# Two token blocks multiplied before their norm, and the second norm's scalings moved behind the residual sums

## The chip, the cores and the metric

The kernel runs on one core of one Trainium2 chip. The metric is the device time of one execution in microseconds; runs before and after are compared by their medians. Each profile is one execution taken by the hardware profiler. Its engines are TensorE (PE; its weight loads are listed apart as PEld), VectorE (DVE), ScalarE (ACT), GpSimd (POOL) and SyncE (SP), and its times count from the first instruction of the span.

## The reference

One decoder layer over 512 tokens of 1024 channels, in float32. What matters here is its beginning and its middle:

```python
u = _rmsnorm(h, norm1_g[l])
proj = u @ w_in[l]
a_glu, q, k, v, r, g_low, gate_a, gate_b = _split_cols(proj)
...
merged = jax.nn.sigmoid(gate_a) * y_conv + jax.nn.sigmoid(gate_b) * y_gla
h = h + merged @ w_o[l]

u2 = _rmsnorm(h, norm2_g[l])
z = _causal_dwconv(u2 @ w_ffn_up[l], ffn_dw_w[l], ffn_dw_b[l])
h = h + (jax.nn.silu(z[..., :FFN_DIM]) * z[..., FFN_DIM:]) @ w_ffn_down[l]
```

`_rmsnorm` multiplies each token by one over the root of its mean square plus 1e-6, and each channel by a gain. The token's factor is common to all channels, so it can be applied to a product's row as well as to the factor that goes into it; the gain can't.

## The kernel before

Tokens lie in four blocks of 128 (`NT` = 4), channels in eight of 128 (`KT` = 8). Every float32 matrix is split in two, a high part (ScalarE casts it to `F32R`: `uh` of activations, `whi` of weights) and a low part, what is left (VectorE subtracts: `ul`, `wlo`). A product takes three TensorE instructions (`mm3`, L288 to L294): activation low by weight high, high by low, high by high. Sums accumulate in PSUM, five banks of tag `mm` and three of tag `ax`. A weight tile is half a megabyte; `load` (L160) issues its DMA on SyncE's queue into one of four `raw` tiles, and `split_weight` (L220) makes `whi` and `wlo` and issues the next load.

**The start** (L377 to L443) runs under an order written out by hand for TensorE, ScalarE, VectorE and SyncE: on each of them instructions stand in the order of the program, and each waits for those ahead. The gain row of the first norm lands on one partition. TensorE spreads it over all partitions with `ones` (L398), makes three products of the identity (L402), and then waits. `norm1` (L404) takes the mean square of a block of tokens on ScalarE (L407), adds 1e-6 on VectorE (L409), the power -0.5 on GpSimd (L340), and scales the block by root and gain in place (L413). `to_channels` (L363) turns the block: four transposes into one PSUM bank (L369), the cast (L373), the subtraction (L374), twice. Then `row_half` (L306) multiplies block 0 by the first half of the value weight (four weight tiles `w_v`, 24 products of 512 columns), then block 1, 2, 3; in the middle of each block (`MID`) the next one is turned and the one after it normalised. `v_done` (L435) copies the values out. The normalised, turned blocks `u1` serve all other input projections, the first of which (`w_glu`) follows at once, by `col_tile` (L296), over all 512 tokens.

**The middle.** The output projection `w_o` goes through `seven` (L816): seven products of sums in place of eight, in the order of `STEPS` (L44), each for two token blocks `i` = 0, 1. A product group of step and `i` is 12 instructions of 512 columns. After a group VectorE adds its bank to the residual `hres` (L859); several steps accumulate into the same bank, so that a later step's group begins only when VectorE has read what stands there. Where a half of `hres` is final, `complete` is called (`o_complete`, L892): the square sum, then the root, then `norm2` (L883), two VectorE instructions that scale a block into `un` (L887). `o_at` (L901) is called just before the addition of its step: at n3 it scaled blocks 0 and 1, at a22 it turned them. The order of instructions in this part isn't written out by hand; a scheduler draws it up from the program's order. The feed-forward part then multiplies its first four `w_up` tiles for 256 tokens (blocks 0 and 1), turns blocks 2 and 3 after the third and the fourth of them (L1016 to L1020), and goes on with the other 256.

## Time and profile before

| | |
|---|---|
| median of 3 runs | 849.79 us (849.37 to 850.01) |
| profiled execution | 850.15 us, of which the span is 848.4 us |
| granted TensorE clock, mean | 0.998 |
| instructions in the span | 9947 |
| DMA | 97.79 MB, mean 115 GB/s |

The profile gives busy time by engine, groups of instructions by line, and for each idle stretch of an engine the one that ended it (`<-`). In a timeline a row is: start, length, engine, line, operation, out<-in, partitions x columns, count, and in brackets the idle time ahead and what ended it. Consecutive instructions of one kind are merged into one row with their count. A product's length includes a tail in which the next one already runs; the distance from start to start is what it costs. A float32 product that isn't `F32R` takes two instructions.

### The profile page before, as it was taken

Reading aid. Unit: us, or ns where it says so; the run is one execution under the profiler, and the core shown is the slowest. Engines: PE = TensorE matmul, PEld = TensorE weight load, DVE = VectorE, ACT = ScalarE, POOL = GpSimd, SP = SyncE. Lnnn points to the kernel's source line nnn. Section 1 sums busy time; section 2 is a strip of 40 time slices with the busy share of each in tenths; the row PEclk is TensorE's granted clock in tenths of the full one; section 3 lists DMA queues with packets and bytes.
Section 4 is the critical chain, followed back from the end, with each engine's and each line's share of the span. In section 5 each row is a group of like instructions: output and inputs, shape, how many; then the busy total and the mean of one; then the engine's idle time right before and its main releaser. Section 6 shows DMA issues by size and latency. Waiting matters only on the chain.

```text
span 848.4 us, 9947 instructions
## 1 busy us (share of the span) xinstructions
PE 835.3 (98%) x3814; PEld 691.0 (81%) x3814; DVE 646.1 (76%) x913; ACT 383.3 (45%) x531; POOL 42.6 (5%) x60
## 2 busy tenths in 40 slices
PE   8999999999999999999999999999999999999996
PEld 6888888888888888788888788888888888888885
DVE  5479879999998788744688749778767777677795
ACT  5433336535443422449444526444334443444454
POOL 1000000000100100000001100000100010000011
PEclk9999999999999999999999999999999999999999
DMA  8223232222222322222338533225732238222462
GB/s 288 94 100 104 95 107 81 97 96 81 94 75 75 124 100 99 75 99 75 119 82 228 191 124 126 100 81 118 211 126 99 71 89 273 96 94 98 100 124 101
DMA packets 28579, 97.79 MB, mean 115 GB/s; under 512 B 3233, under 2 KB 3361, under 8 KB 28530
## 3 DMA queue, kind: packets, MB, share of 16 engines
q1 hardware_dynamic: 25074, 85.35, 28.8%
q0 software_dynamic: 3456, 11.80, 7.8%
q8 instruction: 30, 0.49, 0.2%
q14 instruction: 19, 0.16, 0.1%
HBM read 95.03 MB, written 2.10 MB: 114 GB/s over the span
## 4 chain that ended last, share of the span: by engine, by line
PE 96%; DVE 1%; DMA 1%; ACT 1%; issue 0%; POOL 0%; SPq 0%; POOLq 0%; ACTq 0%
PE mm L292 30%; PE mm L293 29%; PE mm L294 29%; PE ax L293 1%; PE ax L294 1%; PE ax L292 1%; PE ax L698 1%; DMA raw<-in_w_v_dram 1%; PE ax L680 1%; PE ax L700 1%; DVE hres L859 0%; PE ax L369 0%; PE ax L667 0%; PE ax L715 0%; PE ax L666 0%
## 5 line engine op out<-in xcount | busy, mean ns | idle before, releaser
L292 PE MATMUL mm<-uh,wlo 128*128 128x512 f32 (+1 forms) x768 | 294.4, 384 | 1.2 <-DVE wlo L250 0.6
L293 PE MATMUL mm<-ul,whi 128*128 128x512 f32 (+1 forms) x768 | 292.0, 381 | 0.2 <-DVE ul L374 0.2
L294 PE MATMUL mm<-uh,whi 128*128 128x512 f32 (+1 forms) x768 | 292.2, 381 | 0.0
L247 ACT CAST whi<-raw 128x1024 fp32r<-128x1024 f32 x116 | 120.8, 1045 | 134.6 <-PE mm L294 101.3
L250 DVE TENSOR_TENSOR wlo<-raw,whi 128x1024 fp32r<-128x1024 f32 x116 | 141.0, 1219 | 38.3 <-ACT whi L247 37.8
L292 PEld LDWEIGHTS mm<-uh,wlo 128*128 128x128 f32 x768 | 144.2, 188 | 29.0 <-ACT uh L373 1.0
L293 PEld LDWEIGHTS mm<-ul,whi 128*128 128x128 f32 x768 | 144.5, 188 | 27.8 <-DVE ul L374 0.6
L294 PEld LDWEIGHTS mm<-uh,whi 128*128 128x128 f32 x768 | 144.4, 188 | 27.9
L457 DVE SCALAR_TENSOR_TENSOR c<-h,pp,c 128x511 f32<-128x511 f32 (+14 forms) x240 | 162.3, 728 | 0.7
L925 DVE SCALAR_TENSOR_TENSOR tmp<-mm,pp,tmp 128x511 f32<-128x511 f32 x88 | 65.8, 748 | 66.0 <-ACT tmp L923 64.8
L923 ACT ACTIVATE tmp<-mm,pp 128x512 f32<-128x512 f32 x44 | 34.3, 780 | 62.9 <-PE mm L294 62.9
L231 ACT CAST whi<-kept 128x1024 fp32r<-128x1024 f32 (+1 forms) x32 | 31.6, 992 | 24.4 <-DVE kept L211 12.8
L232 DVE TENSOR_TENSOR wlo<-kept,whi 128x1024 fp32r<-128x1024 f32 (+1 forms) x32 | 36.6, 1152 | 2.8 <-ACT whi L231 2.8
L859 DVE TENSOR_TENSOR hres<-hres,mm 128x512 f32<-128x512 f32 x48 | 32.6, 682 | 5.6 <-PE mm L294 3.8
L231 ACT CAST whi<-raw 128x1024 fp32r<-128x1024 f32 (+1 forms) x24 | 23.6, 992 | 19.8 <-PE mm L294 19.5
L340 POOL TENSOR_TENSOR rstd<-var,mhalf 128x1 f32<-128x1 f32 (+1 forms) x20 | 17.6, 884 | 262.2 <-DVE var L705 195.6
L232 DVE TENSOR_TENSOR wlo<-raw,whi 128x1024 fp32r<-128x1024 f32 (+1 forms) x24 | 27.3, 1152 | 3.5 <-ACT whi L231 3.5
L292 PE MATMUL mm<-whi,ul 128*128 128x512 f32 x64 | 26.3, 411 | 1.3 <-DVE ul L374 1.3
L293 PE MATMUL mm<-wlo,sh 128*128 128x512 f32 x66 | 26.0, 395 | 0.0
L294 PE MATMUL mm<-whi,sh 128*128 128x512 f32 x66 | 26.0, 394 | 0.0
L292 PE MATMUL mm<-whi,sl 128*128 128x512 f32 x66 | 25.9, 394 | 0.0
L292 PE MATMUL mm<-h,wlo 128*128 128x512 f32 x64 | 25.7, 402 | 0.0
(220 smaller groups left out, 1124.4 us busy)
## 6 DMA issues: line engine op xcount, KB each, us to landing
raw<-in_w_up_dram SPq DMA_DIRECT2D x44, 512.0 KB, 3.3
raw<-in_w_glu_dram SPq DMA_DIRECT2D x16, 512.0 KB, 3.6
raw<-in_w_down_dram SPq DMA_DIRECT2D x15, 512.0 KB, 3.2
kept<-in_w_down_dram POOLq DMA_DIRECT2D x10, 512.0 KB, 5.1
raw<-in_w_v_dram SPq DMA_DIRECT2D x8, 512.0 KB, 3.9
raw<-in_w_qk_dram SPq DMA_DIRECT2D x8, 512.0 KB, 3.2
raw<-in_w_r_dram SPq DMA_DIRECT2D x8, 512.0 KB, 3.3
raw<-in_w_gb_dram SPq DMA_DIRECT2D x8, 512.0 KB, 3.3
```

Of the source, the lines that this page charges most:

```text
L231: nc.scalar.copy(hi, raw)
L232: nc.vector.tensor_tensor(lo, raw, hi.bitcast(F32), ALU.subtract)
L247: nc.scalar.copy(hi, raw)
L250: pace[0] = nc.vector.tensor_tensor(lo, raw, hi.bitcast(F32), ALU.subtract)
L292: nc.tensor.matmul(acc, ll, rh, start=first, stop=False, **kw)
L293: nc.tensor.matmul(acc, lh, rl, start=False, stop=False, **kw)
L294: nc.tensor.matmul(acc, lh, rh, start=False, stop=last, **kw)
L340: nc.gpsimd.tensor_tensor(r, v, mhalf[:, :n], ALU.pow)
L457: nc.vector.scalar_tensor_tensor(y[:, s:], c[:, : T - s], w, y[:, s:], ALU.mult, ALU.add)
L859: nc.vector.tensor_tensor(hres[t, n], hres[t, n], bank[of[step]][i], op)
L923: nc.scalar.activation(z, acc, AF.Identity, bias=pp[:, PP_FB + m : PP_FB + m + 1], scale=w[2])
L925: nc.vector.scalar_tensor_tensor(z[:, s:], acc[:, : T - s], w[j], z[:, s:], ALU.mult, ALU.add)
```

## The change

Five parts.

1. *The gain row.* It is no longer spread over the partitions. Eight one-column products with a single `1.0` turn it into a tile `gains` of channels by partition.
2. *Blocks 0 and 1* (`EARLY` = 2) are turned as they land. The gain is applied by VectorE while it copies the turned block out of PSUM, the parts are cast and subtracted into tiles of their own (`eu`), and the value product is made of these. The token's factor is applied when `v_done` copies the values out. For the later projections, `normalize` multiplies the turned copies by the factor, spread over the partitions by TensorE, and splits them again into `u1`.
3. *Blocks 2 and 3* are scaled by their factor on ScalarE, turned, and given the gain on the way out of PSUM.
4. *The order* of the first value products is written out: high by high first, then high by low, then low by high; blocks 0 and 1 side by side through the four weight tiles, then block 2, then 3. The first two weight tiles are split in halves of 512 columns. `WARM` now counts products of `ones` at four places of TensorE's queue. The loads stand in the order row, block 0, weight 0, block 1, weights 1 and 2, block 2, weight 3.
5. *The second norm.* The scaling of blocks 0 and 1 moves from ahead of the residual's addition in step n3 to behind it, one block behind each addition; their transposes move one product group ahead, to n3's second group and a22's first; in the feed-forward part blocks 2 and 3 are turned after the second and third `w_up` tile.

```diff
@@ -35,8 +35,9 @@
 AHEAD = 4
 LOOK = 2
 RATE = 5.0
-WARM = 3
+WARM = (6, 6, 6, 4)
 MID = 4
+EARLY = 2
 ET = mybir.EngineType
 SEVEN = {"w_o": KT // 2, "w_down": FT // 2}
 
@@ -217,7 +218,8 @@
             nxt = block(name, pairs, d, *((0, 1) if step == "a11" else (1, 0)))
             nc.gpsimd.dma_start(kept[pairs, d], nxt, accum_op=ALU.add)
 
-    def split_weight(between=None):
+    def split_weight(halves=False, between=None):
+
         if len(ready) < len(order):
             while len(raws) <= len(ready):
                 load()
@@ -244,9 +246,17 @@
                 load()
                 return
             lo = wp.tile([P, D], F32R, tag="wlo", name=nm("wlo"), bufs=4)
+            if halves:
+                ready.append((hi, lo))
+
+                def low(c):
+                    nc.vector.tensor_tensor(lo[:, c], raw[:, c], hi[:, c].bitcast(F32), ALU.subtract)
+
+                cols = [slice(j * T, (j + 1) * T) for j in range(2)]
+                for c in cols:
+                    nc.scalar.copy(hi[:, c], raw[:, c])
+                return [lambda c=c: low(c) for c in cols]
             nc.scalar.copy(hi, raw)
-            if between:
-                between()
             pace[0] = nc.vector.tensor_tensor(lo, raw, hi.bitcast(F32), ALU.subtract)
             ready.append((hi, lo))
             load()
@@ -374,72 +384,211 @@
             nc.vector.tensor_tensor(ul, tr3, uh.bitcast(F32), ALU.subtract)
 
 
+
+
     u1 = new_acts()
-    row = tp.tile([P, D], F32, tag="gain", name=nm("row"), bufs=1)[0:1, :]
+    acts1 = by_k(u1)
     nc.vector.memset(ones, 1.0)
     nc.gpsimd.memset(mhalf, -0.5)
-    xs = {}
+    xs, rs, xg, eu = {}, {}, {}, {}
 
     def load_x(t):
         xs[t] = tp.tile([P, D], F32, tag="x", name=nm("x"), bufs=3)
         nc.sync.dma_start(xs[t], a["x"][t * P : (t + 1) * P, :])
 
+    def by_four(t):
+        return t.rearrange("p (k t) -> p k t", k=4)
+
     start = tc.manual_schedule(engines=START)
     start.__enter__()
+    row = tp.tile([P, D], F32, tag="gain", name=nm("row"), bufs=1)[0:1, :]
     nc.sync.dma_start(row, a["norm1_g"].unsqueeze(0))
     load_x(0)
     load()
-    load()
     load_x(1)
     load()
-
-    gain1 = [mm_bank(), mm_bank()]
-    for j in range(2):
-        nc.tensor.matmul(gain1[j], ones[0:1, :], row[:, j * T : (j + 1) * T], start=True, stop=True)
-
-    warm = ax_bank()
-    for _ in range(WARM):
-        nc.tensor.matmul(warm[:, :P], ident, ident, start=True, stop=True)
-
-    def norm1(t):
-        xt = xs[t]
+    load()
+    load_x(2)
+    load()
+
+    idle = mm_bank()
+
+    def warm(n):
+        for _ in range(n):
+            nc.tensor.matmul(idle[:, :P], ones, ones, start=True, stop=True)
+
+
+    gains = cp.tile([P, KT], F32, name="gains")
+    warm(WARM[0])
+    for k in range(KT):
+        nc.tensor.matmul(
+            idle[:, P + k : P + k + 1], row[:, k * P : (k + 1) * P], ones[0:1, 0:1], start=True, stop=True
+        )
+    nc.scalar.copy(gains, idle[:, P : P + KT])
+    warm(WARM[1])
+
+    def transposed(x, g):
+        tr = ax_bank()
+        for k in range(4):
+            c = (g * 4 + k) * P
+            nc.tensor.transpose(tr[:, k * P : (k + 1) * P], x[:, c : c + P], ident)
+        return tr
+
+    def with_gain(tr, g):
+        f = heap()
+        by_channel = gains[:, g * 4 : g * 4 + 4].unsqueeze(2).to_broadcast([P, 4, P])
+        nc.vector.tensor_tensor(by_four(f), by_four(tr), by_channel, ALU.mult)
+        return f
+
+    def in_u1(t, g):
+        return [x[:, :, t * P : (t + 1) * P] for x in u1[g]]
+
+    def high(hi, f):
+        nc.scalar.copy(hi, f)
+
+    def low(lo, f, hi):
+        nc.vector.tensor_tensor(lo, f, hi.bitcast(F32), ALU.subtract)
+
+    def squares(t):
         ss = small(1, "ss")
-        nc.scalar.activation(junk(D), xt, AF.Square, scale=1.0 / 32.0, accum_out=ss)
+        nc.scalar.activation(junk(D), xs[t], AF.Square, scale=1.0 / 32.0, accum_out=ss)
+        rs[t] = ss
+
+    def root(t):
         v = small(1, "var")
-        nc.vector.tensor_scalar(v, ss, EPS, None, ALU.add)
-        r = rsqrt(v, 1)
-        for j in range(2):
-            s = slice(j * T, (j + 1) * T)
-            nc.vector.scalar_tensor_tensor(xt[:, s], xt[:, s], r, gain1[j], ALU.mult, ALU.mult)
-
-    norm1(0)
-    split_weight()
-    split_weight(lambda: to_channels(xs[0], u1, 0, (0,)))
-    to_channels(xs[0], u1, 0, (1,))
-    load_x(2)
-    norm1(1)
-    split_weight()
+        nc.vector.tensor_scalar(v, rs[t], EPS, None, ALU.add)
+        rs[t] = tp.tile([P, 1], F32, tag="r1", name=nm("r1"), bufs=NT)
+        nc.gpsimd.tensor_tensor(rs[t], v, mhalf[:, :1], ALU.pow)
+
+    def early_acts(t):
+        for g in range(2):
+            xg[t, g] = transposed(xs[t], g)
+
+    def early_gain(t, g):
+        xg[t, g] = with_gain(xg[t, g], g)
+        eu[t, g] = [by_four(heap(F32R)) for _ in range(2)]
+
+    def early_high(t, g):
+        high(eu[t, g][0], by_four(xg[t, g]))
+
+    def early_low(t, g):
+        low(eu[t, g][1], by_four(xg[t, g]), eu[t, g][0])
+
+    def into_u1(t, fs):
+        for g in range(2):
+            high(in_u1(t, g)[0], fs[g])
+        for g in range(2):
+            hi, lo = in_u1(t, g)
+            low(lo, fs[g], hi)
+
+    def normalize(t, r):
+
+        fs = [by_four(xg[t, g]) for g in range(2)]
+        for f in fs:
+            nc.vector.tensor_tensor(f, f, r[:, t * P : (t + 1) * P].unsqueeze(1).to_broadcast([P, 4, P]), ALU.mult)
+        into_u1(t, fs)
+
+    def scale(t):
+        nc.scalar.activation(xs[t], xs[t], AF.Copy, scale=rs[t])
+
+    def late_acts(t, trs):
+        into_u1(t, [by_four(with_gain(tr, g)) for g, tr in enumerate(trs)])
+
+
+    vt = {}
+
+    def v_done(t, n, acc):
+        vt[t, n] = heap()
+        if n == 0 and t < EARLY:
+            nc.scalar.activation(vt[t, n], acc, AF.Copy, scale=rs[t])
+        else:
+            nc.scalar.copy(vt[t, n], acc)
+
+    ws = [order[j] for j in range(KT // 2)]
+    assert ws == [("w_v", j) for j in range(KT // 2)]
+    used[0] = len(ws)
+
+    HH, HL, LH = (0, 0), (0, 1), (1, 0)
+
+    def by_parts(acc, t, ks, parts=(HH, HL, LH)):
+
+        for wi, ai in parts:
+            for k in ks:
+                act = eu[t, k // 4][ai][:, k % 4, :] if t < EARLY else acts1[k][ai][:, t * P : (t + 1) * P]
+                j = slice((k % 2) * T, (k % 2 + 1) * T)
+                first, last = k == 0 and (wi, ai) == HH, k == KT - 1 and (wi, ai) == LH
+                nc.tensor.matmul(acc, act, ready[k // 2][wi][:, j], start=first, stop=last)
+
+    accs = [mm_bank() for _ in range(EARLY)]
+    early_acts(0)
+    early_gain(0, 0)
+    early_gain(0, 1)
+    early_high(0, 0)
+    warm(WARM[2])
+    lows = split_weight(True)
+    early_low(0, 0)
+    for low_half in lows:
+        low_half()
+    by_parts(accs[0], 0, (0, 1), (HH,))
+    early_acts(1)
+    squares(0)
+    by_parts(accs[0], 0, (0, 1), (HL, LH))
+    warm(WARM[3])
+    early_gain(1, 0)
+    lows = split_weight(True)
+    early_high(1, 0)
+    for low_half in lows:
+        low_half()
+    load()
+    early_low(1, 0)
+    early_high(0, 1)
+    by_parts(accs[0], 0, (2, 3), (HH, HL))
+    by_parts(accs[1], 1, (0, 1), (HH,))
+    by_parts(accs[0], 0, (2, 3), (LH,))
+    by_parts(accs[1], 1, (0, 1), (HL, LH))
+    by_parts(accs[1], 1, (2, 3))
+    early_low(0, 1)
+    early_gain(1, 1)
     split_weight()
     load_x(3)
-    acts1 = by_k(u1)
-
-    def next_tokens(t):
-        if t + 1 < NT:
-            to_channels(xs[t + 1], u1, t + 1)
-        if t + 2 < NT:
-            norm1(t + 2)
-
-
-    vt = {}
-
-    def v_done(t, n, acc):
-        vt[t, n] = heap()
-        nc.scalar.copy(vt[t, n], acc)
-
-    def values(n, middle):
-        row_half("w_v", n * KT // 2, n, acts1, KT, v_done, n == 1, middle)
-
-    values(0, next_tokens)
+    early_high(1, 1)
+    early_low(1, 1)
+    for t in range(EARLY):
+        by_parts(accs[t], t, (4, 5))
+    squares(2)
+    root(2)
+    split_weight()
+    root(0)
+    scale(2)
+    squares(1)
+    root(1)
+    by_parts(accs[0], 0, (6, 7))
+    trs = [transposed(xs[2], g) for g in range(2)]
+    by_parts(accs[1], 1, (6, 7))
+    late_acts(2, trs)
+    squares(3)
+    root(3)
+    v_done(0, 0, accs[0])
+    v_done(1, 0, accs[1])
+    scale(3)
+
+    spread_r = ax_bank()
+    for t in range(EARLY):
+        to = spread_r[:, t * P : (t + 1) * P]
+        nc.tensor.matmul(to, rs[t].to_broadcast([P, P]), ident, start=True, stop=True)
+    acc = mm_bank()
+    by_parts(acc, 2, range(4))
+    normalize(0, spread_r)
+    trs = [transposed(xs[3], g) for g in range(2)]
+    late_acts(3, trs)
+    by_parts(acc, 2, range(4, KT))
+    v_done(2, 0, acc)
+    prefetch(1)
+    normalize(1, spread_r)
+    acc = mm_bank()
+    by_parts(acc, 3, range(KT))
+    prefetch(LOOK)
+    v_done(3, 0, acc)
     start.__exit__(None, None, None)
     load_consts()
 
@@ -589,7 +738,7 @@
                 nc.scalar.activation(ab[h], ab[h], AF.Ln, bias=1.0)
                 nc.vector.tensor_tensor(ls[h], ls[h], ab[h], ALU.subtract)
 
-    values(1, gate)
+    row_half("w_v", KT // 2, 1, acts1, KT, v_done, True, gate)
 
 
     def gl(n, tag, bufs):
@@ -893,19 +1042,17 @@
         square_sum(("n2", t), hres[t, n], n)
         if n == (0 if t > 1 else 1):
             roots[t] = total_rstd(("n2", t))
-            if t > 1:
-                normed[t] = norm2(t, roots[t])
+        if t > 1:
+            done = t if n == 0 else t - 2
+            normed[done] = norm2(done, roots[done])
 
     u2 = []
 
     def o_at(step, i):
-        if (step, i) == ("n3", 0):
-            for t in range(2):
-                normed[t] = norm2(t, roots[t])
-        if (step, i) == ("a22", 0):
+        if (step, i) == ("n3", 1):
             u2.extend(new_acts())
             to_channels(normed[0], u2, 0)
-        if (step, i) == ("a22", 1):
+        if (step, i) == ("a22", 0):
             to_channels(normed[1], u2, 1)
 
     seven("w_o", O_PAIRS, mixed, o_complete, o_at)
@@ -1016,8 +1163,8 @@
             for lo in (0, T // 2):
                 for j, (w, acc) in enumerate(zip(ws, accs)):
                     col_tile(w, acts2, acc, lo, lo + T // 2)
-                    if lo == 0 and j > 1:
-                        to_channels(normed[j], u2, j)
+                    if lo == 0 and j in (1, 2):
+                        to_channels(normed[j + 1], u2, j + 1)
             early = {pairs[0][0]: accs[:2], pairs[0][1]: accs[2:]}
 
         def both(i):
```

## The prediction

> **What bounds the kernel now.** I read the list of what TensorE waited for first, then the timeline of its first 20 us, the chain of waits around 470 to 492 us, and the timeline there.
>
> ```profile
> PE 835.3 (98%) x3814; PEld 691.0 (81%) x3814; DVE 646.1 (76%) x913; ACT 383.3 (45%) x531; POOL 42.6 (5%) x60
> ...
> PE mm L398 <- DMA row<-in_norm_g_dram: 2.3, 1, 2.3
> PE mm L292 <- DVE ul L374: 1.3, 1, 1.3
> PE mm L292 <- DVE hres L859: 1.2, 1, 1.2
> PE mm L292 <- DVE wlo L250: 0.6, 1, 0.6
> PE mm L292 <- ACT uh L373: 0.5, 2, 0.3
> PE mm L293 <- DVE ul L374: 0.2, 1, 0.2
> ```
>
> The reader is to see that TensorE's queue is the time: its six waits are 6.1 us together, 3.6 of them before the first sum, 2.5 around the second norm. Those are the two places that the change edits; whatever either gains or loses arrives at the end undiminished, since TensorE stands nowhere else for long enough to absorb it.
>
> The first place:
>
> ```profile
> 0.90 0.17 DVE L379 MEMSET ones<- 128x128 f32 x1 [0.90 <-PEq L1110]
> 2.33 3.75 PE L398 MATMUL mm<-row,ones 1*128 1x512 f32 x4 [2.33 <-DMA row<-in_norm_g_dram]
> 4.49 1.06 ACT L407 ACTIVATE junk<-x 128x1024 bf16<-128x1024 f32 x1 [2.40 <-DMA x<-in_x_dram]
> 5.84 1.05 ACT L247 CAST whi<-raw 128x1024 fp32r<-128x1024 f32 x1 [0.20 <-DMA raw<-in_w_v_dram]
> 6.00 1.65 PE L402 MATMUL ax<-ident 128*128 128x128 f32 x6
> 7.44 1.92 PE L369 MATMUL ax<-ident,x 128*128 128x128 f32 x8
> 8.32 1.05 ACT L247 CAST whi<-raw 128x1024 fp32r<-128x1024 f32 x1 [1.43 <-DMA raw<-in_w_v_dram]
> 10.63 0.79 PE L292 MATMUL mm<-whi,ul 128*128 128x512 f32 x1 [1.27 <-DVE ul L374]
> ...
> 14.64 0.62 PE L292 MATMUL mm<-whi,ul 128*128 128x512 f32 x1
> 15.06 0.42 PE L293 MATMUL mm<-wlo,uh 128*128 128x512 f32 x1
> ...
> 15.56 1.03 PE L369 MATMUL ax<-ident,x 128*128 128x128 f32 x8
> ...
> 19.20 0.39 PE L292 MATMUL mm<-whi,ul 128*128 128x512 f32 x1
> 19.42 0.39 PE L293 MATMUL mm<-wlo,uh 128*128 128x512 f32 x1
> 37.31 0.39 PE L292 MATMUL mm<-uh,wlo 128*128 128x512 f32 x1
> ```
>
> Block 0 of the tokens has landed by 4.49 and the first weight by 5.84, yet the first sum starts at 10.63: norm, transposes, cast and subtraction stand in a row between. And until about 15.1 TensorE runs at half rate: a 512-column product follows the last after 0.42 us (14.64 to 15.06), later after 0.227 (19.20, 19.42). The windows show a granted clock of 1.00 all the while, so the rate is read from these steps. At 37.31 the first product of the next projection starts; that is the end of the stage.
>
> **The first stage after the change.** TensorE's queue now holds 44 warm-up pieces (22 products of `ones`, two pieces each, as the six pieces of L402 are three products), 16 pieces that turn the gain row to channels, 32 transposes, 96 products and 4 pieces that spread the inverse roots. Fast prices: 0.109 us for a transpose (row 15.56: eight in 1.03 with 0.16 of tail), and for the small pieces
>
> ```profile
> 368.44 0.79 PE ax L487 x8
> ```
>
> 0.10 us for a one-column piece. At half rate the pieces of L402 take 1.65 us for six with a tail of 0.37, 0.213 each, so 0.107 at the full one: a one-column piece is about as dear as a 128-column one, and I price it at 0.213 when slow. At the fast rate the queue is 44 x 0.11 + 16 x 0.10 + 32 x 0.109 + 96 x 0.227 + 4 x 0.11 = 4.8 + 1.6 + 3.5 + 21.8 + 0.4 = 32.1 us. It can begin at 1.1 (the `ones` are there at 0.90 + 0.17; `row` at 2.33, under the first twelve pieces). Its waits: the first product needs four transposes, a gain product, a cast, and a cast of half a weight behind it:
>
> ```profile
> 16.19 1.08 ACT L373 CAST uh<-ax 128x512 fp32r<-128x512 f32 x2 [2.92 <-PE ax L369]
> 16.81 1.29 DVE L374 TENSOR_TENSOR ul<-ax,uh 128x512 fp32r<-128x512 f32 x2
> ```
>
> A 512-column operation takes 0.69 us on VectorE and 0.59 on ScalarE; 0.69 + 0.59 + 0.59 with hand-overs is about 2.0 after the fourth transpose, and four transposes and twelve pieces cover 0.44 + 1.3, so some 0.5 with the second half; further on some 0.3. All at full rate, the stage would end at 1.1 + 32.1 + 0.8 = 34.0 against 37.31.
>
> The rest is the clock. Each microsecond at half rate does half a microsecond's work, so with the rate rising at F the stage ends at 34.0 + (F - 1.1)/2, and it breaks even with 37.31 at **F = 7.7**. When does it rise? Before, 1.65 us of identity products followed by transposes did not raise it; 4.43 us of sums (10.63 to 15.06) did. Halfway is 3.0 us of full-array work. If all that TensorE does counts, F = 1.1 + 3.0 = 4.1. If the one-column pieces don't count, the first twelve pieces give 2.56 (to 3.66), the row takes 16 x 0.213 = 3.4 (to 7.07), and the missing 0.44 comes at F = 7.5. No row tells them apart; I take the middle, **F = 5.8**, and with it an end at 36.35: **-1.0 us**. Bounds: F = 2.75 (1.65 us suffice after all) gives 34.8, -2.5; the far end is the last rival.
>
> The Trainium skill ("TensorE: Matmul & The Clock Gate", Part 1) has the clock rise after a busy window of some 3.4 us that runs free of the kernel's start, and Part 4 says that transposes don't count as busy. The 4.43 us here fit such a window. By these rules a first stretch of 2.56 us fills no window, and F comes far later: the last rival.
>
> Costed at nothing. **Squares, roots and scalings** of ScalarE move behind the sums; four squares, four roots and the value copies stay as many as before, and only blocks 2 and 3 get a pass of 1.05 us each, on an engine that is under half used. **VectorE** gets two more products and two more subtractions for each early block (4 x 0.6 us), and ScalarE two more casts, to write the normalised copy that later projections read: under the sums of blocks 2 and 3. The tightest piece is block 1: behind block 2's copy on ScalarE stand a weight's cast (1.05), its subtraction (1.2), two products (1.2), casts (0.5) and two subtractions (1.2), some 5.1 us, while block 3 sums for 24 x 0.227 = 5.4. If the cover fails, the next projection starts up to 0.5 late. **Loads**: block 1 moves ahead of the second weight and block 2 ahead of the fourth on SyncE's queue; at the 387 GB/s of this stretch
>
> ```profile
> 8.00:10.00 2.00, 1.36 (x7) 0.95 (x5) 1.23 (x2) 1.68 (x3) 0.00 (x0) 1.00 0.97 387
> ```
>
> half a megabyte takes 1.35 us. The second weight, cast at 8.32 before, comes at about 9.7 and is first used after 13; the fourth is needed near 19. Block 3's load waits for the square of block 0 and has the later weights of the next projection behind it in SyncE's queue; these are read after 37. Two transposed groups more in PSUM turn through the same three banks, each freed by its gain product.
>
> **The second norm.** The timelines of TensorE and VectorE:
>
> ```profile
> 480.15 0.27 PE L369 MATMUL ax<-ident,un 128*128 128x128 f32 x1
> 481.59 0.48 PE L292 MATMUL mm<-whi,h 128*128 128x512 f32 x1 [1.18 <-DVE hres L859]
> 481.91 0.40 PE L293 MATMUL mm<-wlo,h 128*128 128x512 f32 x1
> ...
> 488.02 1.47 PE L369 MATMUL ax<-ident,un 128*128 128x128 f32 x12
> 489.80 0.50 PE L292 MATMUL mm<-uh,wlo 128*128 128x256 f32 x2 [0.31 <-ACT uh L373]
> 490.92 0.39 PE L292 MATMUL mm<-uh,wlo 128*128 128x256 f32 x1 [0.62 <-DVE wlo L250]
> 491.52 0.39 PE L293 MATMUL mm<-ul,whi 128*128 128x256 f32 x1 [0.22 <-DVE ul L374]
> 491.74 0.29 PE L294 MATMUL mm<-uh,whi 128*128 128x256 f32 x1
> 491.87 0.28 PE L292 MATMUL mm<-uh,wlo 128*128 128x256 f32 x1
> ...
> 503.21 1.03 PE L369 MATMUL ax<-ident,un 128*128 128x128 f32 x8
> 504.48 0.75 PE L292 MATMUL mm<-uh,wlo 128*128 128x256 f32 x4 [0.24 <-ACT uh L373]
> 505.20 0.39 PE L293 MATMUL mm<-ul,whi 128*128 128x256 f32 x1
> ```
>
> ```profile
> 479.44 1.41 DVE L887 SCALAR_TENSOR_TENSOR un<-hres,rstd,gain 128x512 f32<-128x512 f32 x2 [0.45 <-POOL rstd L340]
> 480.77 0.68 DVE L859 TENSOR_TENSOR hres<-hres,mm 128x512 f32<-128x512 f32 x1
> ```
>
> The bank that step a22 adds to must first be read by `hres` (L859). That read stood behind block 1's scaling, itself waiting for a root until 479.44. TensorE started a transpose at 480.15 and the next product at 481.59: 1.44 less 0.11 is 1.33 lost. At 488.02 twelve transposes (1.31) and three 256-column products of 0.12 should have reached 489.69; the row of products after them begins at 491.52, 1.83 lost, because block 1's transposes came only after a22's second half. At 503.21 eight transposes and four products (0.87 + 0.48) should have reached 504.56; 505.20 was 0.64 late, since block 3's second group is read at once. Together 3.8 us.
>
> Now the sums come first on VectorE and each scaling behind them: the 1.33 goes, as the read needs 0.68 after a product group that ends near 477.5, and block 0's scaling (1.41) still ends before n3's second group does near 480.1. Block 1 is turned one product group (12 x 0.227 = 2.7 us) earlier, which covers its cast and two subtractions (1.08 + 1.29): most of the 1.83 goes. Block 3 gets a whole 24 x 0.12 = 2.9 us of cover: the 0.64 goes. What stays: a first product behind transposes comes 0.1 late even with all ready (481.59 to 481.91 in place of 0.227), at some five places, and the order that the scheduler draws up in this part is not in the diff. I take **-2.7 us**; bounds -3.3 and -0.5 (a scaling that is late in its new place, where transposes now stand ahead of a22 and hold the whole queue).
>
> **Sum.** -1.0 - 2.7 = -3.7. The profiled execution took 850.15 for a span of 848.4, so 846.45; it is 0.36 above the median of the runs, which a clock that rises 0.7 us earlier would explain, and for which I take nothing off: **846.4 us**.
>
> **Rivals.**
>
> *The gain row breaks the warm-up* (24%). The clock counts only an unbroken run, and the 3.4 us of one-column pieces break it; it rises from the second stretch on, which begins at 7.07 and runs through transposes: F = 7.07 + 3.0 = 10.1, end 38.5, +1.2 for the stage, 848.65 in all. For it speaks that 3.75 us of one-row products before 6.08 did nothing visible for the rate; against it, that no row shows whether broken runs add up.
>
> *The second norm keeps its wait* (12%). VectorE has 10.76 of 12 us busy there:
>
> ```profile
> 480.00:492.00 12.00, 9.68 (x53) 7.56 (x52) 10.76 (x17) 8.27 (x17) 0.55 (x1) 1.00 0.47 170
> ```
>
> Reordering doesn't shorten its list, and TensorE may stand for block 0's scaling where it stood for the sum. Then -0.5 in place of -2.7: 848.65. Against it: part of what VectorE waited for there, the 0.45 ahead of 479.44, was a root, and a sum doesn't wait for one.
>
> *Slower: the rate rises only in the midst of the sums* (14%). Neither transposes nor one-column pieces count, and a pause starts the count anew. At half rate the transposes of block 0 take 9.63 to 11.34, twelve warm-ups and two products 3.4 us to 14.75, block 1's transposes reach 16.46; four products, eight warm-ups and the sums then run on, and F = 16.46 + 3.0 = 19.5. By then the waits are gone: 33.2 + 18.4/2 = 42.4, +5.1, and with -2.7 852.55. With the second norm as forecast it makes the kernel slower than 849.79 from F = 14.0 on. The rows of 6.00 and 7.44 speak for it (identity products and transposes back to back for 3.4 us, and the rate stayed low); the thing against it is that the 1.65 us of products among them may just be too few. This is what the two rules of the Trainium skill named above come to.
>
> **How the numbers follow.** Forecast 50% (844.9 to 848.2 for F from 3.5 to 8 and -3.3 to -2.2 at the second norm), then 24, 12 and 14. A measurement of this kernel tells about 0.2% from no change, 1.7 us: faster is below 848.1, slower above 851.5. Faster: 48 of the forecast's 50, 8 of the first rival's 24, 2 of the second's 12: 0.58. Slower: 11 of the last's 14: 0.11. The rest, 0.31, is the same. Range 844.6 to 850.9; the likeliest case's own is 844.9 to 848.2.
>
> **What would show it.** The step from one sum to the next falls from 0.43 to 0.23 us at about 6 us, and the first product of the next projection starts near 36.3; a fall after 7.7 makes the stage no gain, one after 14 a loss. Near 480 TensorE waits for no `hres`, and from the end of a22 to the up-projection's products there is under half a microsecond. I am wrong if the first sum still runs at half rate, or if TensorE stands for `un` or `uh` at step a22.

## The result, and the profile after

The changed kernel takes 847.08 us (median of 7 runs, 846.66 to 847.48) against 849.39 us before (7 runs, 848.75 to 850.01): 0.9971 of the time, 95% interval 0.996 to 0.9983. That is 2.3 us faster, where 3.4 against the earlier median were forecast, and the time lies in the range. The steps behind the forecast don't bear it out, though: the start became 5 us slower instead of 1 us faster, and the total came right by luck, because something gained that the forecast didn't know.

First the list of TensorE's waits after the change, with the line of busy times:

```profile
PE 834.8 (99%) x3868; PEld 697.7 (83%) x3868; DVE 649.9 (77%) x923; ACT 388.0 (46%) x540; POOL 41.5 (5%) x60
...
PE mm L302 <- ACT uh L447: 1.3, 1, 1.3
PE mm L418 <- DVE ones L391: 1.1, 1, 1.1
PE mm L418 <- ACT gains L427: 0.3, 1, 0.3
PE ax L434 <- ACT x L492: 0.2, 1, 0.2
PE mm L303 <- DVE ul L450: 0.2, 1, 0.2
```

The waits of the second norm (`hres`, `wlo`, `uh` L373) are gone, and all that is left lies in the first 43 us. The waits fell from 6.1 to 3.1 us, and the span from 848.4 to 845.3. That the two differences agree is chance, as it shows when one asks at what time each kernel reaches the same instructions. These are the products of one line of `mm3`, grouped by operand, with count, shortest/median/longest in ns, and the start of the first and the last in us; before:

```profile
L292 PE MATMUL mm<-uh,wlo x768: 278/389/580, 37.3 to 801.6; 128*128 128x512 f32 x176, 128*128 128x256 f32 x16
L292 PE MATMUL mm<-h,wlo x64: 390/393/794, 289.9 to 356.6; 128*128 128x512 f32 x64
L292 PE MATMUL mm<-whi,sums x32: 389/389/398, 455.5 to 479.5; 128*128 128x512 f32 x32
L292 PE MATMUL mm<-whi,yl x44: 390/394/404, 581.6 to 835.1; 128*128 128x512 f32 x44
```

and after:

```profile
L302 PE MATMUL mm<-uh,wlo x768: 277/389/582, 41.8 to 799.0; 128*128 128x512 f32 x176, 128*128 128x256 f32 x16
L302 PE MATMUL mm<-h,wlo x64: 389/389/795, 294.7 to 360.3; 128*128 128x512 f32 x64
L302 PE MATMUL mm<-whi,sums x32: 389/389/389, 458.5 to 482.3; 128*128 128x512 f32 x32
L302 PE MATMUL mm<-whi,yl x44: 389/389/389, 580.5 to 831.7; 128*128 128x512 f32 x44
```

| at | after less before, us | gained or lost since the row above |
|---|---|---|
| end of the start (third product of `w_glu`: 37.31 + 2 x 0.227 = 37.76 before, 42.84 after) | +5.1 | +5.1 |
| first product of `h,wlo` (290) | +4.8 | -0.3 |
| last product of `h,wlo` (357) | +3.7 | -1.1 |
| last product of `whi,sums` (480), ahead of the second norm's scalings | +2.8 | -0.9 |
| first product of `whi,yl` (582) | -1.1 | -3.9 |
| last product of `whi,yl` (835) | -3.4 | -2.3 |

There are three entries, not two: the start (+5.1), the second norm (-3.9), and a slow drift of -4.6 in parts that the diff doesn't touch. Where it drifts, the shortest and median durations fell as well: a product with `yl` took 390 ns at the least and 394 in the median, now 389 throughout.

**The start.** TensorE's timeline, in the columns of the earlier ones:

```profile
1.12 2.93 PE L418 MATMUL mm<-ones 128*128 128x128 f32 x12 [1.12 <-DVE ones L391]
3.98 3.57 PE L424 MATMUL mm<-ones,row 1*128 1x1 f32 x16
7.80 2.93 PE L418 MATMUL mm<-ones 128*128 128x128 f32 x12 [0.25 <-ACT gains L427]
10.52 1.73 PE L434 MATMUL ax<-ident,x 128*128 128x128 f32 x8
12.08 1.50 PE L418 MATMUL mm<-ones 128*128 128x128 f32 x12
13.61 1.02 PE L520 MATMUL mm<-whi,h 128*128 128x512 f32 x2
...
38.54 1.98 PE L520 MATMUL mm<-wlo,uh 128*128 128x512 f32 x8
41.77 0.51 PE L302 MATMUL mm<-uh,wlo 128*128 128x512 f32 x1 [1.26 <-ACT uh L447]
42.50 0.51 PE L303 MATMUL mm<-ul,whi 128*128 128x512 f32 x1 [0.22 <-DVE ul L450]
42.84 0.40 PE L304 MATMUL mm<-uh,whi 128*128 128x512 f32 x1
```

Twelve pieces (six products) of `ones` take 2.93 us at 1.12 and again at 7.80, and 1.50 at 12.08: the rate rose just ahead of that row (the trace's record of the rate has 11.92). At the other end, the eight products from 38.54 are through at 38.54 + 8 x 0.227 = 40.36. The first of `w_glu` starts at 41.77, the second and third 0.73 and 0.34 later where 0.23 is due: 2.0 us lost. ScalarE and VectorE at that place:

```profile
37.38 1.05 ACT L259 CAST whi<-raw 128x1024 fp32r<-128x1024 f32 x1 [1.68 <-PE mm L520]
39.24 1.23 DVE L260 TENSOR_TENSOR wlo<-raw,whi 128x1024 fp32r<-128x1024 f32 x1 [3.66 <-PE mm L520]
40.39 1.28 DVE L488 TENSOR_TENSOR h<-h,ax 128x512 f32<-128x512 f32 x2
41.10 1.22 ACT L447 CAST uh<-h 128x512 fp32r<-128x512 f32 x2 [2.68 <-DVE h L488]
41.75 1.29 DVE L450 TENSOR_TENSOR ul<-h,uh 128x512 fp32r<-128x512 f32 x2
```

`normalize(1)` is the `h` row (L488) and the `uh` and `ul` rows behind it (L447, L450). Ahead of it in both queues stands `prefetch(1)`, which splits the next weight; its cast waits for block 3's sums (1.68), its subtraction 3.66, since all four `whi` and `wlo` tiles are still read by them. VectorE idles 3.66 us with finished input for block 1 behind the waiting instruction.

**The second norm.** VectorE's timeline, then TensorE's:

```profile
481.70 0.68 DVE L1008 TENSOR_TENSOR hres<-hres,mm 128x512 f32<-128x512 f32 x1
482.29 1.41 DVE L1036 SCALAR_TENSOR_TENSOR un<-hres,rstd,gain 128x512 f32<-128x512 f32 x2
```

```profile
482.94 1.03 PE L379 MATMUL ax<-ident,un 128*128 128x128 f32 x8
483.73 0.48 PE L302 MATMUL mm<-whi,h 128*128 128x512 f32 x1
```

The sum is read at 481.70, ahead of block 1's scaling, and the products follow the transposes without a wait: 482.94 + 8 x 0.109 = 483.81 was due, and 483.73 came.

### The profile page after: what moved, and what is told of

It is laid out like the page before. It is cut to its first block, busy times and chain, and to the rows that moved or that the text cites. A ratio compares the mean times of both kernels' runs of the same rounds, so it can differ in the third digit from the quotient of the medians.

```text
span 845.3 us, 10064 instructions
## 1 busy us (share of the span) xinstructions
PE 834.8 (99%) x3868; PEld 697.7 (83%) x3868; DVE 649.9 (77%) x923; ACT 388.0 (46%) x540; POOL 41.5 (5%) x60
## 4 chain that ended last, share of the span: by engine, by line
PE 96%; DVE 2%; ACT 1%; issue 0%; POOL 0%; POOLq 0%; ACTq 0%; DVEq 0%
PE mm L302 28%; PE mm L304 28%; PE mm L303 28%; PE mm L520 2%; PE mm L418 1%; PE ax L847 1%; PE ax L304 1%; PE ax L302 1%; PE ax L303 1%; PE ax L829 1%; PE ax L849 1%; PE ax L434 1%; DVE hres L1008 0%; DVE wlo L260 0%; PE ax L816 0%; PE mm L424 0%
## 5 line engine op out<-in xcount | busy, mean ns | idle before, releaser
L259 ACT CAST whi<-raw 128x1024 fp32r<-128x1024 f32 x114 | 118.7, 1045 | 130.7 <-PE mm L304 97.4
L260 DVE TENSOR_TENSOR wlo<-raw,whi 128x1024 fp32r<-128x1024 f32 x114 | 138.6, 1219 | 36.0 <-ACT whi L259 32.2
L350 POOL TENSOR_TENSOR rstd<-var,mhalf 128x2 f32<-128x2 f32 (+1 forms) x16 | 14.2, 896 | 241.0 <-DVE var L854 196.4
L302 PE MATMUL mm<-ch,wlo 128*128 128x512 f32 x64 | 25.1, 393 | 0.0
```

The lines of the kernel that those rows point to most:

```text
L259: nc.scalar.copy(hi, raw)
L260: pace[0] = nc.vector.tensor_tensor(lo, raw, hi.bitcast(F32), ALU.subtract)
L302: nc.tensor.matmul(acc, ll, rh, start=first, stop=False, **kw)
```

## The experiments

Medians of each batch stand beside a median of before taken with it on the same chip: 849.94 for the first four kernels, 849.61 for the others.

### The drift: three kernels on absolute place, all without effect

The first idea for the shorter products was that tiles had moved to better addresses. A small unused tile ahead of all others moves everything behind it.

```diff
+    pad = cp.tile([P, 8], F32, name="pad")       # pad32, after_pad32
+    pad = cp.tile([P, 16], F32, name="pad")      # pad64
...
+    nc.gpsimd.memset(pad, 0.0)
```

`pad32`, before with 32 bytes in each partition:

> The kernel before with 32 bytes more per partition at the end of its constants; every tile allocated behind them moves by 32 bytes, as the changed kernel's 8-column gain tile moves them, and no other instruction changes but one clear of 32 bytes on GpSimd. Theory A (place): the changed kernel's shorter steps after 235 us (0.227 in place of 0.232 us for products of tiles h, sh, yh, ah) come from where its tiles lie; then those steps are 0.227 here too and the time falls by about 4.5 us (849.4 to 844.9). Theory B (order): they come from the changed order of the start; then nothing moves, within 0.8 us of before.

Measured 850.28 us, ratio 1.0008 (0.9999 to 1.0016).

`pad64`, before with 64 bytes:

> The same with 64 bytes: a control. Theory A, if the place counts by multiples of 64 bytes: no change, 849.4 within 0.8. Theory A, if any move helps or the absolute place counts: some other step, between -4.5 and +4.5. Theory B: no change.

Measured 850.33 us, ratio 1.0004 (0.9995 to 1.0013).

`after_pad32`, the change with 32 bytes:

> The changed kernel with 32 bytes more, so that its tiles begin at multiples of 64 bytes again as before the change. Theory A: the steps on h, sh, yh and ah go back to 0.232 us and the time rises by about 4.5 us to 851.6, above the kernel before. Theory B: 847.1 within 0.8.

Measured 847.81 us, ratio 0.997 (0.9957 to 0.9983), like the change. Absolute place by steps of 32 bytes does nothing that these intervals can tell from zero. But these pads moved weights and activations together, so they said nothing of the distance between them.

### The second norm alone

`s2_only` is before with part 5 of the diff and nothing else.

> The kernel before with the second norm's edit alone; its tiles lie where they lay before. Reading of the two traces: the distance between them falls from +2.8 to -1.1 us there, so 3.9 us less than before, 845.5, and TensorE has no wait between 470 and 500 us. The prediction's term was -2.7, 846.7. If the gain belongs to the place of the tiles or needs the new start, less than 2 us.

Measured 846.0 us (845.4 to 846.11), ratio 0.9954 (0.9942 to 0.9966): -3.9. Its list of waits has the gain row's and one more, both of the start:

```profile
...
PE mm L292 <- DVE ul L374: 1.2, 1, 1.2
```

So part 5 is worth 3.9 us by itself, as much as the table has between 480 and 582 us, and gives nothing of the drift.

### The distance between weights and activations

Parts 1 to 4 add four tiles of one column, the roots `r1`, each of which takes 32 bytes of a partition. They stand between the weight tiles and the activations' heap: by the program's layout the first `whi` and the first heap tile lie 99,456 bytes apart before and 99,584 after, 128 more. `gap128` puts four unused tiles there in before; `all160` moves weights and heap both by 160 bytes, which brings the heap to the address that it has after the change, with the old distance; `after_nogap` is the change with its roots in an existing tag, which takes the 128 bytes away.

```diff
+    for _ in range(NT):                                                     # gap128
+        gap = tp.tile([P, 1], F32, tag="gap", name=nm("gap"), bufs=NT)
+        nc.gpsimd.memset(gap, 0.0)
...
+    pad = cp.tile([P, 40], F32, name="pad")                                 # all160
...
-        rs[t] = tp.tile([P, 1], F32, tag="r1", name=nm("r1"), bufs=NT)      # after_nogap
+        rs[t] = small(1, "rstd")
```

> The kernel before with four unused 32-byte tiles in its pool of temporaries, so that everything behind them (the heap, the feed-forward tiles) moves 128 bytes away from the weight tiles, as the changed kernel's four root tiles move it; 32 and 64 bytes that moved weights and heap together changed nothing. Theory C (distance): products with an operand there step at 0.227 in place of 0.232 us because of its distance from the weight tiles; time falls by about 4.5 us to 845.4. Theory D (absolute place): also falls, if 125760 lies on the fast side; the kernel all160 tells C from D. Theory B (the order of the start): no change, 849.9 within 0.8.

> The kernel before with 160 bytes more at the end of its constants: the heap lies where the changed kernel's lies (125792), and the weights moved along, so that their distance is that of before. Theory C (distance): no change, 849.9 within 0.8, steps at 0.232. Theory D (absolute place): 845.4, steps at 0.227. Theory B: no change.

> The changed kernel with its four inverse roots in the tiles that the later norms use anyway, so that heap and weights have the distance of before. Theories C and D: steps on heap and feed-forward operands at 0.232, time up by about 4.5 us to 851.6, above the kernel before; that is what the change is worth by itself, +5.1 at the start and -3.9 at the second norm. Theory B: 847.1 within 0.8.

| kernel | distance, bytes | us | ratio to before |
|---|---|---|---|
| `gap128` | 99,584 | 845.54 | 0.9948 (0.9933 to 0.9963) |
| `all160` | 99,456 | 850.6 | 1.0007 (0.9997 to 1.0016) |
| `after_nogap` | 99,456 | 851.94 | 1.0024 (1.0008 to 1.0039) |

The products of `yh` by line and tile (durations and starts as above), of before, `gap128`, `all160`, the change and `after_nogap`, one row each:

```profile
L293 PE MATMUL mm<-wlo,yh x44: 390/393/404, 581.9 to 835.3; 128*128 128x512 f32 x44
```

```profile
L293 PE MATMUL mm<-wlo,yh x44: 389/389/389, 579.1 to 830.3; 128*128 128x512 f32 x44
```

```profile
L294 PE MATMUL mm<-wlo,yh x44: 390/393/404, 582.3 to 835.7; 128*128 128x512 f32 x44
```

```profile
L303 PE MATMUL mm<-wlo,yh x44: 389/389/389, 580.8 to 831.9; 128*128 128x512 f32 x44
```

```profile
L303 PE MATMUL mm<-wlo,yh x44: 390/393/404, 583.3 to 836.7; 128*128 128x512 f32 x44
```

The two with the greater distance have 389 throughout, the three with the smaller one 390 to 404, whatever else was changed. From the first of these products to the last it takes 253.4 us in before, `all160` and `after_nogap`, and 251.2 and 251.1 in `gap128` and the change. The products of `h` say the same. Their rows of before and the change stand above; here are those of `gap128` and `after_nogap`:

```profile
L292 PE MATMUL mm<-h,wlo x64: 389/389/798, 288.5 to 354.1; 128*128 128x512 f32 x64
```

```profile
L302 PE MATMUL mm<-h,wlo x64: 390/393/795, 294.8 to 361.5; 128*128 128x512 f32 x64
```

That is 65.6 and 66.7 us, with 65.6 in the change and 66.7 before. So the 128 bytes are worth 2.3 + 1.1 = 3.4 us in these two stretches, and with another 0.3 in the traces of `gap128` and the change between 447 and 480 us it is 3.7.

The other 0.9 us of the drift are not this distance. The 0.3 ahead of 290 us stands in `after_nogap` too. Another 0.4 arises from 403 to 447 us, among products of the tiles `ch` and `c`, which follow no such rule: there the change and `all160` gain 0.4 on before, while `gap128` loses 0.2 and `after_nogap` 0.4. This is a row of `all160`:

```profile
L293 PE MATMUL mm<-ch,wlo x64: 389/389/389, 403.6 to 446.9; 128*128 128x512 f32 x64
```

Before and `gap128` have 394 in the median here, and the change 393. The program puts `ch` in a pool on the other side of the memory (`"right"`), so a pad ahead of the weights presumably changes the distance between the two; no run tests it.

In the medians, four unused tiles alone gain 4.1 us, but not all of it is the distance. In the profile of `gap128` the rate also rose early (9.60 us against 15.11 before), and its `w_glu` starts at 36.03 in place of 37.31. The change without the 128 bytes is 2.3 us **slower** than before in the medians, and 1.8 in the profiles' spans: 5.2 lost at the start, 3.9 gained at the second norm, and 0.4 lost elsewhere. That is the measured value of what the diff says it does. Its start differs little from the change's: the third product of `w_glu` comes at 43.00, there at 42.84.

### The start: the order of two lines, then the products of ones

`norm_first` puts block 1's normalising ahead of the weight split.

```diff
-    prefetch(1)
     normalize(1, spread_r)
+    prefetch(1)
```

> The changed kernel with block 1's normalising ahead of the next projection's weight split on ScalarE's and VectorE's queues. Reading of the trace: the split waits for a weight tile that block 3's sums free only at 37.2 us, and the normalising stands behind it, so that the first products of w_glu come 1.4 + 0.5 us late. Expected -1.9 us, 845.2, and no wait of TensorE for uh (L447) there. Rival: something else is late next (the weight split itself): -0.5 or less.

Measured 845.39 us (842.84 to 846.98), ratio 0.9947 (0.9929 to 0.9966): 1.7 less than the change, with intervals that just overlap. The trace is clearer: no wait for `uh` or `ul` is left in TensorE's list, and of the 2.0 us lost ahead of `w_glu` 0.3 is left (its third product comes at 38.66, where 38.35 was due). VectorE's timeline now reads

```profile
34.42 1.29 DVE L450 TENSOR_TENSOR ul<-h,uh 128x512 fp32r<-128x512 f32 x2
36.79 3.50 DVE L260 TENSOR_TENSOR wlo<-raw,whi 128x1024 fp32r<-128x1024 f32 x3 [1.08 <-PE mm L520]
```

with block 1 done at 35.7 (43.0 in the change), and only the weight's split waiting. The rate gave a part of these 7.3 us, as the same profile happens to show. Stretches of 3.41 us, with busy time of PE, PEld, DVE, ACT, POOL, then the granted clock (0.50 is half rate), DMA share and GB/s; and TensorE's timeline:

```profile
4.08:7.49 3.41, 3.15 (x27) 3.07 (x28) 0.00 (x0) 0.17 (x1) 0.00 (x0) 1.00 1.03 411
7.49:10.90 3.41, 3.41 (x18) 3.41 (x18) 1.85 (x3) 1.21 (x3) 0.00 (x0) 0.50 1.03 420
10.90:14.30 3.40, 3.40 (x26) 3.08 (x26) 3.02 (x6) 3.40 (x7) 0.00 (x0) 1.00 0.47 146
```

```profile
3.98 1.97 PE L424 MATMUL mm<-ones,row 1*128 1x1 f32 x16
6.21 1.79 PE L418 MATMUL mm<-ones 128*128 128x128 f32 x12 [0.26 <-ACT gains L427]
7.79 1.91 PE L434 MATMUL ax<-ident,x 128*128 128x128 f32 x8
```

Here the first twelve pieces of `ones` had raised the rate at 4.08; the sixteen one-column pieces took 1.97 us in place of 3.57. But at 7.49 the rate fell back to half, though TensorE had been busy for 3.15 of the last 3.41 us. Of those only 6.21 to 7.49 were products of the whole array, 1.28 us or 38%. The one-column pieces, which fill TensorE's row, did not hold the rate.

`norm_first_warm6` and `trim` are `norm_first` with other counts of products of `ones`.

```diff
-WARM = (6, 6, 6, 4)
+WARM = (6, 0, 0, 0)     # norm_first_warm6
+WARM = (0, 0, 3, 0)     # trim
```

> norm_first with only the first six products of ones; the sixteen products behind the gain row, after the transposes and in the sums are gone (WARM 6, 0, 0, 0). If the later ones only take TensorE's time: 1.5 to 2.5 us less than norm_first, 843 to 844. If they are what brings the rate up: it rises a window or more later and the time is as norm_first's or up to 2 us more, 845 to 847.5.

Measured 842.83 us (841.86 to 844.09), ratio 0.9922 (0.991 to 0.9935): 2.6 less than `norm_first`, though in its profile the rate rose only at 15.17.

> norm_first with no products of ones ahead of the gain row nor behind it, three after the transposes of block 0 (WARM 0, 0, 3, 0): the transposes start once the gain row is through. If the stage is as long as the work put in TensorE's queue and half the time before the rate rises: 3 to 4 us less than norm_first, 841.5 to 842.5. If the products of ones at the start bring the rate up: it rises after 13 us, and the time is 844 or more.

Measured 840.2 us (839.89 to 840.79), ratio 0.9891 (0.9877 to 0.9904), 5.2 less than `norm_first`. Its start:

```profile
2.32 3.54 PE L424 MATMUL mm<-ones,row 1*128 1x1 f32 x16 [2.32 <-DMA row<-in_norm_g_dram]
5.79 1.97 PE L434 MATMUL ax<-ident,x 128*128 128x128 f32 x8
7.55 1.49 PE L418 MATMUL mm<-ones 128*128 128x128 f32 x6
8.94 1.31 PE L520 MATMUL mm<-whi,h 128*128 128x512 f32 x2
...
35.46 0.50 PE L302 MATMUL mm<-uh,wlo 128*128 128x512 f32 x1
```

The transposes of block 0 start at 5.79 in place of 10.52, the first sum at 8.94 in place of 13.61, and `w_glu` at 35.46 in place of 41.77. The rate rose at 10.54 in this profile, no later than with 19 products of `ones` more. So here the work itself raised it; the products of `ones` cost what they take of the queue, at half rate for the most part.

### The old start with the rest

`old_start` is before with part 5 and the four unused tiles. `old_start_fill` adds three products of `ones` where TensorE waits for the first `ul`.

```diff
     to_channels(xs[0], u1, 0, (1,))
+    for _ in range(3):
+        nc.tensor.matmul(warm[:, :P], ones, ones, start=True, stop=True)
```

> The old start, with the second norm's edits and with four unused 32-byte tiles that set the activations 128 bytes further from the weights. If the change's gain comes from these two alone, and its new start costs time: 849.6 - 3.9 - 4.1 = 841.6, under the change by 5. If the two overlap (the spacing already accounts for a part of what the second norm's edits gave): about 844. If the new start is worth its 1 us as forecast: 846 or more.

Measured 841.61 us (840.84 to 842.19), ratio 0.9909 (0.9893 to 0.9924). The two gains add up to the tenth, which is partly luck: in this profile too the rate rose early (9.32), and `w_glu` starts at 35.66 in place of 37.31. The old start with both is 5.5 us faster than the change. Against `trim` it is 1.4 slower, and no run of the one reaches the other's (840.79 against 840.84). How much of this is the start isn't shown: in the profiles `w_glu` starts at 35.66 and 35.46, 0.2 apart, and 0.6 of the difference arises between 403 and 447 us, at `ch` and `c`.

> old_start with three products of ones (six pieces) in the 1.3 us in which TensorE waits for the first sum's low part, so that it is busy without a break from the identity products on. If transposes count for the rate: it rises one window of 3.4 us earlier in most executions, 1 to 1.7 us less than old_start, about 840.2. If transposes don't count: as old_start, or 0.1 more.

Measured 840.97 us (840.85 to 842.3), ratio 0.9902 (0.9889 to 0.9916). The 0.6 under `old_start` lies inside both intervals, and in the profiles of both the rate had risen by the first sum (9.32 and 10.08), so the filling wasn't put to the test. This one is inconclusive.

## Why the prediction was right in its total and wrong in its steps

| step | forecast, us | measured, us | by |
|---|---|---|---|
| start | -1.0 | +5.1 | third product of `w_glu` |
| second norm | -2.7 | -3.9 | `s2_only`, and the table above |
| distance of the operands | no term | -3.7 | stretches of the table, against `gap128` and `after_nogap` |
| rest of the drift | no term | -0.9 | the same |
| sum | -3.7 | -3.4 | spans: 848.4 to 845.3, -3.1 |

**The work of the start** was priced right: 32.1 us at the full rate. The stage ends at 42.84 - 2 x 0.227 = 42.39, of which 1.12 is the beginning, some 4.8 the half rate and some 4.3 lost at hand-overs (both counted from the steps of all products in the trace), which leaves about 32.2.

**"I take the middle, F = 5.8"** failed. The rate rose at 11.92, and 4.8 us went to it, not 2.35. The step took the count as one of unbroken work, somewhere between two guesses. The rows show fixed stretches of 3.41 us (4.08, 7.49, 10.90 in `norm_first`), and a stretch counts only if products of the whole array or transposes fill most of it: 67% was too little, and 84% was enough (`norm_first`, where products of `ones` fill 1.12 to 3.98 of the stretch that ends at 4.08). In the change's profile, counted back from 11.92, these begin at 1.68, 5.09 and 8.50. The first has 3.98 - 1.68 = 2.30 us of `ones`, 67%, and then one-column pieces: no rise. The second is mostly one-column pieces. The third is full of `ones` and transposes, and the rate rises. That one-column pieces break the warm-up is what the first rival supposed; its F = 10.1 was nearer than the forecast.

That transposes count is shown by `gap128`:

```profile
6.15 1.65 PE L405 MATMUL ax<-ident 128*128 128x128 f32 x6
7.59 1.91 PE L369 MATMUL ax<-ident,x 128*128 128x128 f32 x8
10.29 0.50 PE L292 MATMUL mm<-whi,ul 128*128 128x512 f32 x1 [0.78 <-DVE ul L374]
10.62 0.39 PE L293 MATMUL mm<-wlo,uh 128*128 128x512 f32 x1
10.86 0.39 PE L294 MATMUL mm<-whi,uh 128*128 128x512 f32 x1
```

The first sums already follow at 0.24 (10.62 to 10.86), where before they took 0.42 as late as 14.64. The stretch that did it, 6.19 to 9.60, holds 1.40 us of products (41%, less than the 67% that failed) and transposes for nearly all the rest. The forecast had read from the same instructions before the change that they are too little. Counted back from 15.11, a stretch there ends at 8.28, in the midst of the transposes: the work was enough, but lay in two stretches, with 67% in the first. By the Trainium skill ("TensorE: Matmul & The Clock Gate", Part 4) transposes don't count as busy; the measurement differs, and it decides. The Trainium skill (the same page, Part 1) has a free-running window of 3413 ns, and the 3.41 here agrees. Together the two rules gave F = 19.5, the last rival.

**"If the cover fails, the next projection starts up to 0.5 late"** failed by four times: 2.0. The list in that step was complete (a weight's cast and its subtraction stood in it ahead of block 1), and each was priced by its duration. None was asked what it waits for: a tile that block 3's last sums free, the very work that was to be the cover. `norm_first` shows it: the same instructions behind `normalize(1)` let block 1 through at 35.7. Another 1.5 of the 4.3, beyond the 0.8 that had been priced, are small hand-overs (0.39 at the copy of the gains, 0.40 ahead of block 3's transposes).

**Loads costed at nothing** held: no wait for a load stands in the list after the change. So did squares and roots; of the scalings, block 3's on ScalarE (L492) cost TensorE a wait of 0.2, a part of the 0.40 above.

**The second norm** was right in its mechanism and too small in its size, beyond its bound of -3.3. All 3.8 us of the waits went, and the 0.1 that was kept for each of five places behind transposes did not fall due (483.73 above is one of them).

**What decided the sign had no term.** Nothing in the forecast asked where the new tiles would lie. Without their 128 bytes the kernel is at 851.94, within a microsecond of the last rival's 852.55. The end of that rival's stage, 42.4, was met to the tenth, and that is luck as well: the rate rose earlier than the rival had it, and waits that it took for gone made up for that. What the forecast named as proof against it, a first sum still at half rate, did not come (13.61, two in 1.02), and the step was wrong all the same; the start of `w_glu`, forecast for 36.3, was the sign that told.

What stays open is why the distance matters: only two distances were run, and the 128 bytes stand between the activations and all that lies ahead of them, of which the weights are one part. Open too is whether they move the rate. In all three profiles with the unused tiles and the old start it rose at 9.3 to 10.1, in five without them at 14.1 to 15.1; eight profiles can't tell chance from cause, and of the runs without a profile it isn't known.

## What to carry to other kernels

Price an instruction that stands ahead of critical work by what it waits for as well as by how long it takes: a weight split that needs a tile still in use blocks the queue for as long as the work that is meant to hide it. A product that only warms the array takes the queue as long as one that computes; of three kernels here that differ in nothing else (`norm_first`, `norm_first_warm6`, `trim`), the one with the fewest was the fastest, and in its profile the real work raised the rate. Where products that nobody touched change their length between two kernels, compare where their operands lie before crediting the edit.

## What the runs showed of the hardware

- A 512-column product with an operand on the heap or in the feed-forward tiles took 389 ns throughout, or 390 to 404, by how far that operand lies from the weights: 128 bytes more, on some 99 KB of a partition, made 3.7 us of 850. Moving both by 160 bytes left these products as they were (`all160`).
- TensorE's rate changes at the ends of fixed stretches of 3.41 us, in both directions: in the records of all fourteen profiles the last stretch at full rate is 822.61, 826.03, 829.44 or 832.85 us long, whole multiples of 3.413. It fell after a stretch that was busy for 3.15 of 3.41 us, most of it one-column pieces. A stretch with 67% of products didn't raise it, one with 84% did, and so did one of products (41%) and transposes.
- Sixteen one-column pieces of one partition took 1.97 us at the full rate and 3.57 at half: 0.22 each then, about what one of 128 columns takes (twelve in 2.93, 0.24).
